# Joining two bursts of small matmuls per scan unit, with own tiles for one set of weights and three moved steps

## The chip, the core and the metric

The kernel runs on one NeuronCore of one Trainium2 chip. The core has five engines with a queue of instructions each: TensorE (PE: matmuls and transposes; loading of the stationary operand is listed apart as PEld), VectorE (DVE), ScalarE (ACT), GpSimd (POOL) and SyncE (SP, which here only issues DMAs). They run side by side and wait for each other by semaphores. The metric is the device time of one execution in microseconds: the median of the runs.

## The reference: what is computed

One decoder layer. A prompt of 2048 tokens (width 1024) and 8 single new tokens of a sample, which come with states, pass through the same layer:

```python
h = rmsnorm(x, norm_g)
p = h @ w_in                       # 8 groups of 512 columns
rq, rk, rv, rg, hq, hf, hi, hgate = split(p, 8)
# retention, 4 heads of 128: rotary on rq and rk, fixed decay per head, chunks of tokens
# HGRN2, 4 heads of 128: forget gate f = lb + (1 - lb) sigmoid(hf), per key channel
S_t = diag(f_t) S_{t-1} + k_t v_t^T ;  o_t = S_t^T q_t
y = x + concat(headnorm(o_ret) * silu(rg), headnorm(o_hg) * silu(hgate)) @ w_out
return rmsnorm(y, final_norm_g), and the last states
```

All inputs and outputs are float32.

## The kernel before, in words

**Precision.** A large product `x @ w` is made of three matmuls: both operands are split into a rounded half `h` (ACT, line 117) and a remainder `l` (DVE, line 118), and `hh + hl + lh` is accumulated. Small float32 matmuls are written once and appear as two instructions each.

**Start.** `wu` (lines 82 to 86) is a product of ones that nobody reads: 14 wide matmuls of 128 columns and 12 small ones run while the first inputs arrive.

**Value stage** (`v_pair`, line 383 on, and the loop from line 908). For three sets of projection weights (values; rotary q and its gate; rotary k and the HGRN2 gate) eight pairs of 128 tokens are taken through a 2 x 2 block product with seven instead of eight half-size products (operands `S1` to `S4` and `T1` to `T4` are sums and differences). One pair is seven steps of 12 matmuls (128x128 by 512); `after[n]` lists what is issued behind step n, and n + 0.5 means in the middle of the next step. The first two pairs are done plainly (`plain_k`), and `decode_values` multiplies the 8 sample tokens with the raw value weights `wr` in two bursts: k = 0, 1, 4, 5 after `kk = 1`, and k = 2, 3, 6, 7 after `kk = 3`. `four` spreads such a product over four column tiles. Afterwards `w_sums` (lines 502 to 507) turns the raw weights in place into the T operands.

While set 0 or 1 runs, the weights of the next set are prepared in four steps (k = 0 to 3, at pairs j = 2 to 5): `wg_load` asks SP for two pieces of 512 KB into the shared ring `raw` of six buffers, at step 0; `wg_decode` multiplies the sample tokens with them and `wg_spool` makes and stores the sums, both at step 4 (at step 5 in pair 3). The token statistics of later pairs are loaded and summed by `stats_load`, `stats_sum` and `stats_end` (POOL), and spread over partitions by a transpose (`spread`, line 288) that scales the next pair's tokens.

In the last set the retention recurrence runs along in `r_steps` (lines 795 to 828): `r_flip` transposes a chunk of rotated keys (line 726), then `r_score`, `r_update` and `r_out` follow.

**Scan stage** (`hgrn_proj`, `hgrn_rec`, `merge`). Eight units: two halves of 1024 tokens by four HGRN2 heads. The projections of unit i (`seg_steps`, line 1032, steps of six matmuls) are the filling, in which the recurrence of unit i - 1 (`levels`) and the end of unit i - 2 (`rest`) are put at given fractions of its length. A recurrence goes through seven levels of spans (1, 2, 4 ... 64 tokens), whose scores are bursts of tiny 128x32 matmuls: `scores0` (64 instructions, line 1264), `levels2(1)` and `levels2(3)` (128 each, line 1246) and `scores3` (64, lines 1289 and 1297). Between them `update(li)` multiplies keys and queries on DVE (lines 1216 and 1219) by the span products that `products` has made, and `keep` copies them on ACT. After `scores3` the score matrix `A` (one buffer) is completed by ACT; `k0` and `k1` transpose the keys (line 1107), `u0` and `u1` make the state updates, `o0` and `o1` the outputs.

**Output stage** (`out_steps`, `o_pair`). The first four chunks fill the last unit; then six pairs run through seven steps each. The sample's own output is put between them by `wd_at`: `d_ms`, `d_rs` (DVE, line 1392), `d_tr` (a transpose, line 1396) and later the products `wd_mm`.

**Order.** PE's instructions run in the order in which they are written. The other engines' order is found by a planner that simulates the program, with the rule that what stands in `behind(...)` is not issued before the instructions traced last on its engine.

Of the kernel before, what the change touches and what calls it, by code (L numbers as in the profile page):

```python
# [10 lines left out]
F32 = mybir.dt.float32  # L11
# [7 lines left out]
P = 128  # L19
# [22 lines left out]
def step_kernel(ctx, tc, a, out):  # L42
# [40 lines left out]
    for n in range(14):  # L83
        pe.matmul(wu, ones, ones, start=True, stop=True)
    for n in range(12):
        pe.matmul(wu[:32, :16], ones[:, :32], ones[:, :16], start=True, stop=True)
# [415 lines left out]
    def w_sums(r0, r1):  # L502
        dve.tensor_tensor(r0[:, 0], r0[:, 1], r0[:, 0], op=ALU.subtract)
        dve.tensor_tensor(r0[:, 1], r1[:, 1], r0[:, 1], op=ALU.subtract)
        dve.tensor_tensor(r1[:, 1], r1[:, 1], r0[:, 0], op=ALU.subtract)
        dve.tensor_tensor(r1[:, 0], r1[:, 0], r1[:, 1], op=ALU.subtract)
        return ("T2", r1[:, 1]), ("T3", r0[:, 1]), ("T1", r0[:, 0]), ("T4", r1[:, 0])
# [13 lines left out]
    def wg_decode(n, k):  # L521
        if n not in pgd:
            pgd[n] = ps_o.tile([P, 256], F32, tag="o", name=f"pgd{n}")
        for kk in (k, k + 4):
            four(pgd[n], xs[:, kk], wr[kk].rearrange("p a b -> p (a b)"), kk == 0, kk == KT - 1)
# [61 lines left out]
    def four(ps, x, w, first, last):  # L587

        for j in range(4):
            pe.matmul(ps[32 * j : 32 * j + x.shape[1]], x, w[:, j * 256 : j * 256 + 256], start=first, stop=last)  # L590
# [204 lines left out]
    def r_steps(p):  # L795
# [112 lines left out]
    for i in range(2, n_tok):  # L908
# [268 lines left out]
    MOVE = {(0, 0, 1): 0.065, (0, 1, 3): 0.065, (0, 2, 1): 0.065, (1, 0, 1): 0.125, (1, 3, 1): 0.11}  # L1177

    def hgrn_rec(half, h, u):
# [23 lines left out]
        def products():  # L1203
            box["fp"] = pools["ep"].tile([P, HALF], F32, tag="fp", name=f"fp{name}")
            for li in range(len(LEVELS)):
                two = spans(li).rearrange("p (n two) -> p n two", two=2)
                dve.tensor_tensor(spans(li + 1), two[:, :, 0], two[:, :, 1], op=ALU.mult)
            box["dec"] = sm.tile([P, CH], F32, tag="dec", name=f"dec{name}")
            dve.tensor_copy(box["dec"], spans(len(LEVELS)))
# [48 lines left out]
        def scores0():  # L1258
            box["Ab"] = pools["up"].tile([P, CH, 32], F32, tag="Ab", name=f"Ab{name}")
            pa = ps_lv.tile([P, CH, 2, 32], F32, tag="lv", name=f"pa{name}")  # L1260
            for c in range(CH):
                for i in range(4):
                    cc = slice(c * P + 32 * i, c * P + 32 * i + 32)
                    pe.matmul(pa[32 * i : 32 * i + 32, c], k[:, cc], u["qq"][:, :, cc], start=True, stop=True)
            update(0)
# [3 lines left out]
            put(pa[:, :, 1].rearrange("p c (n two b) -> p c n two b", two=2, b=1)[:, :, :, 1, :], 0)  # L1269
            keep(1)  # L1270
# [11 lines left out]
        def scores3():  # L1282
            pl = ps_lv.tile([P, CH // 2, 96], F32, tag="lv", name=f"pl{name}5")
# [9 lines left out]
            for n in range(CH // 2):  # L1293
                for g in range(4):
# [5 lines left out]
                    )  # L1300
            update(6)
# [4 lines left out]
            for e in range(2):  # L1306
                act.activation(A[0:64, e::2, 64:128], pl[64 * e : 64 * e + 64, :, 32:96], AF.Copy)
            for i in range(4):
# [25 lines left out]
        return levels, rest  # L1334
# [228 lines left out]
    levels, rest, late = [], [], []  # L1563
    tail = r_steps(N_V)
    tail_f = [lambda n=n: [f() for f in tail[n]] for n in sorted(tail)]
    for i in range(len(order)):
# [24 lines left out]
        levels, rest = hgrn_rec(*order[i], u)  # L1591
# [285 lines left out]
    wd_at[2] += [(0, d_ms), (2, d_rs), (4, d_tr)]  # L1877
# [103 lines left out]
```

## Time and profile before

| | |
|---|---|
| median of 3 runs | 1027.93 us (1026.58 to 1029.33) |
| the profiled execution | 1030.97 us |
| its span on the core | 1029.1 us |
| granted TensorE clock, mean | 0.998 |
| PE busy | 1014.0 us (99%), 8366 matmuls |
| DVE, ACT, POOL busy | 734.2, 550.3, 122.8 us |
| DMA | 255.63 MB, mean 248 GB/s |

The profile shows one execution. Its times count from the span's start; "idle before" is the time in which an engine did nothing ahead of an instruction, with what ended that wait. Matmuls are pipelined, so a row's length is longer than its distance to the next row; the distance of the starts is what one costs. By the order of time, the last product of the value stage begins at 567.75 us, the projections of the scan (L1032) at 572.75, the first recurrence burst (L1264) at 603.28, and the first product of an output pair (L350) at 901.13.

### The profile page before, as it was taken

The page shows a single profiled execution, that of the slowest core. Times are in us where ns is not written, and L with a number is a line of the kernel's source. Part 1 is how long each engine was busy: PE and PEld are TensorE (multiplying, and loading weights), DVE is VectorE, ACT ScalarE, POOL GpSimd, SP SyncE. Part 2 cuts the span into 40 slices and gives each one's busy share as a digit, 9 for nine tenths or more (in the row PEclk, how much of TensorE's full clock was granted, in tenths as well). Part 3 has the DMA queues.
Part 4 walks back from the last instruction along what each step waited for, and adds up shares of the span by engine and source line. Part 5 has one row for each costly group of instructions (what it writes and reads, how often), then busy time and mean ns, then how long its engine had stood idle before and what let it go on. Part 6 is the DMA issues. An engine that isn't in the chain of part 4 may idle for free.

```text
span 1029.1 us, 21541 instructions
## 1 busy us (share of the span) xinstructions
PE 1014.0 (99%) x8366; PEld 841.7 (82%) x8366; DVE 734.2 (71%) x1353; ACT 550.3 (53%) x1211; POOL 122.8 (12%) x231
## 2 busy tenths in 40 slices
PE   9999999999999999999999999999999999999997
PEld 7767778887778888888888899898888878878775
DVE  7887666888675885576666768768768576667886
ACT  7863435735434765555564665667556476433242
POOL 0200001000000101111111100111022112301122
PEclk9999999999999999999999999999999999999999
DMA  8699998878999965567766697555864496565652
GB/s 290 210 327 330 332 334 275 326 263 313 312 326 304 359 238 184 189 226 247 233 222 205 210 334 268 193 185 200 283 216 133 129 362 227 180 252 204 227 186 103
DMA packets 151271, 255.63 MB, mean 248 GB/s; under 512 B 11424, under 2 KB 79280, under 8 KB 151040
## 3 DMA queue, kind: packets, MB, share of 16 engines
q1 hardware_dynamic: 141408, 225.03, 64.7%
q0 software_dynamic: 7440, 24.76, 6.3%
q10 hardware_dynamic: 2320, 4.46, 1.2%
q8 instruction: 66, 1.08, 0.4%
q14 instruction: 37, 0.30, 0.1%
HBM read 166.51 MB, written 87.69 MB: 247 GB/s over the span
## 4 chain that ended last, share of the span: by engine, by line
PE 82%; DMA 4%; DVE 1%; issue 0%; SPq 0%; POOLq 0%; ACT 0%; POOL 0%; DVEq 0%; ACTq 0%
PE po L350 10%; PE pjqh L1032 9%; PE pjfh L1032 8%; PE py L1659 4%; PE plh L1246 2%; PE pur L741 1%; PE par L734 1%; PE puh L1115 1%; PE por L747 1%; PE por L749 1%; PE poh L1131 1%; DMA oT1h<-t_dramh 1%; PE poh L1133 1%; PE pv20a L350 1%; PE pv21a L350 1%; PE pv22a L350 1%
## 5 line engine op out<-in xcount | busy, mean ns | idle before, releaser
L1032 PE MATMUL pjfh<-xh,w_h 128*128 128x512 f32 (+2 forms) x160 | 59.4, 372 | 0.0
L1032 PE MATMUL pjqh<-xh,w_h 128*128 128x512 f32 (+2 forms) x160 | 58.9, 368 | 0.0
L1226 ACT ACTIVATE kepth<-kh 128x1024 f32<-128x1024 f32 x24 | 25.4, 1060 | 62.0 <-DVE kh L1216 62.0
L1032 PE MATMUL pjqh<-xh,w_l 128*128 128x512 f32 (+2 forms) x160 | 55.7, 348 | 0.0
L1032 PE MATMUL pjfh<-xh,w_l 128*128 128x512 f32 (+2 forms) x160 | 55.7, 348 | 0.0
L1032 PE MATMUL pjfh<-xl,w_h 128*128 128x512 f32 (+2 forms) x160 | 55.6, 348 | 0.0
L1032 PE MATMUL pjqh<-xl,w_h 128*128 128x512 f32 (+2 forms) x160 | 55.6, 347 | 0.0
L1216 DVE TENSOR_TENSOR kh<-kh,fph 128x512 f32<-128x512 f32 x48 | 33.4, 696 | 22.8 <-PE plh L1246 19.8
L118 DVE TENSOR_TENSOR ab_l<-xr,ab_h 128x512 fp32r<-128x512 f32 (+1 forms) x40 | 37.5, 954 | 11.6 <-ACT ab_h L117 11.6
L772 DVE SCALAR_TENSOR_TENSOR obr<-por,omr,rg 128x128 f32<-128x128 f32 x64 | 18.0, 344 | 33.3 <-POOL omr L764 28.2
L762 ACT ACTIVATE obr<-por 128x128 f32<-128x128 f32 x64 | 16.8, 277 | 44.4 <-PE por L749 40.6
L117 ACT ACTIVATE ab_h<-xr 128x512 fp32r<-128x512 f32 (+1 forms) x40 | 32.4, 838 | 11.3 <-DVE xr L302 11.3
L1032 PEld LDWEIGHTS pjqh<-xh,w_h 128*128 128x128 f32 x160 | 30.4, 190 | 4.8 <-issue 1.2
L1032 PEld LDWEIGHTS pjfh<-xh,w_h 128*128 128x128 f32 x160 | 30.2, 189 | 4.1 <-issue 0.4
L1032 PEld LDWEIGHTS pjqh<-xh,w_l 128*128 128x128 f32 x160 | 30.1, 188 | 4.1
L1032 PEld LDWEIGHTS pjfh<-xh,w_l 128*128 128x128 f32 x160 | 30.1, 188 | 4.0
L409 ACT ACTIVATE vo<-vo 128x512 f32<-128x512 f32 x32 | 20.1, 629 | 24.7 <-DVE vo L403 10.8
L1219 DVE TENSOR_TENSOR qqh<-qqh,fph 128x512 f32<-128x512 f32 x48 | 32.8, 683 | 0.0
L1032 PEld LDWEIGHTS pjqh<-xl,w_h 128*128 128x128 f32 x160 | 30.2, 189 | 3.0
L1032 PEld LDWEIGHTS pjfh<-xl,w_h 128*128 128x128 f32 x160 | 30.2, 189 | 2.7
L302 DVE SCALAR_TENSOR_TENSOR xr<-xr,g_in,rb 128x256 f32<-128x256 f32 x64 | 27.1, 480 | 7.3 <-DMA xr<-in_x_t 4.2
L1659 PE MATMUL py<-woh,oc_h 128*128 128x512 f32 x64 | 26.6, 415 | 0.0
(1839 smaller groups left out, 3335.0 us busy)
## 6 DMA issues: line engine op xcount, KB each, us to landing
xr<-a_dram SPq DMA_DIRECT2D x24, 512.0 KB
S<-s_dram SPq DMA_DIRECT2D x24, 512.0 KB
xn<-in_x_prompt SPq DMA_DIRECT2D x32, 256.0 KB
xr<-in_x_t SPq DMA_DIRECT2D x16, 512.0 KB
a_dram<-xr SPq DMA_DIRECT2D x16, 512.0 KB
s_dram<-S SPq DMA_DIRECT2D x16, 512.0 KB
wgr<-in_w SPq DMA_DIRECT2D x16, 512.0 KB
xr<-a_dram SPq DMA_DIRECT2D x32, 256.0 KB
```

Of the source, the lines that this page charges most:

```text
L117: act.activation(h, src, AF.Copy)
L118: dve.tensor_tensor(l, src, h.bitcast(F32), op=ALU.subtract)
L302: dve.scalar_tensor_tensor(r[:, k], r[:, k], g_in[:, kk : kk + 1], spread_to[i], op0=ALU.mult, op1=ALU.mult)
L350: pe.matmul(ps, xx, ww, start=(first and n == 0), stop=(last and n == 2), skip_group_check=more)
L409: act.activation(o, src, AF.Silu)
L772: dve.scalar_tensor_tensor(o[:, cc], po[:, h], ms[:, h : h + 1], rb_of[c, "g"][:, cc], op0=ALU.mult, op1=ALU.mult)
L1032: pe.matmul(ps, ww[:, kk], x[:, k, b0 : b0 + n], start=(k == 0 and i == 0), stop=(k == KT - 1 and i == 2),)
L1216: dve.tensor_tensor(kv[:, :, 0, :], kv[:, :, 0, :], two[:, :, 1:2].to_broadcast([P, nb, b]), op=ALU.mult)
L1219: dve.tensor_tensor(qv[:, :, 1, :], qv[:, :, 1, :], two[:, :, 0:1].to_broadcast([P, nb, b]), op=ALU.mult)
L1226: act.activation(ss[:, 512:], k[:, :HALF], AF.Copy)
L1246: pe.matmul(dst[32 * i : 32 * i + 32, c], kk, qq, start=True, stop=True)
L1659: pe.matmul(ps, o[:, kk], w[:, k % 4, i * 512 : (i + 1) * 512], start=(k == 0 and n == 0), stop=(k == KT - 1 and n == 2),)
```

## The change

Six edits:

- Warm-up: 5 wide matmuls and 59 with 8 columns, for 14 and 12 with 32 columns.
- `decode_values` for all eight k in one burst after `kk = 3`.
- Raw weights of the first prepared set (`n == 1`): for even k both pieces, for odd k the second piece go to tiles that already exist in the pool `vq` (`zh0`, `zl0`, `zh1`, `zl1`, and `rk`, `rg`), each piece as two DMAs of half a row. They are asked for earlier, k = 0 behind step 1 of pair 2 and k = 1 to 3 behind step 5 of pairs 2 to 4; `wg_decode` and `wg_spool` of this set move from step 4 to step 6.
- `stats_sum(i + 2, 0)` and `stats_load(i + 2, 1)` at step 1 for every pair; `r_flip(0)`, `r_score(0)` and `r_update(0)` half a step later; `d_tr` from step 4 of output pair 2 to step 0 of output pair 3.
- Scan: `scores3` of a unit is issued directly ahead of the matmuls of the next unit's `scores0`. Its end (`update(6)` and the copies into `A`) is issued behind them, ahead of `update(0)`; `k0` and `k1` follow at 0.13 and 0.16, `u0` and `u1` at 0.27 and 0.35. The copies of `Ab` into `A` go behind `levels2(3)`. The last unit keeps its own `scores3`.
- Scan, with it: the two uppermost span products are made after `scores0` (`FIRST = 5`) in one lasting tile `fp`; the places of `levels2` change (`AT`, `MOVE`).

```diff
-    for n in range(14):
+    for n in range(5):
         pe.matmul(wu, ones, ones, start=True, stop=True)
-    for n in range(12):
-        pe.matmul(wu[:32, :16], ones[:, :32], ones[:, :16], start=True, stop=True)
+    for n in range(59):
+        pe.matmul(wu[:8, :16], ones[:, :8], ones[:, :16], start=True, stop=True)
...
     def wg_load(n, k):
-        for kk in (k, k + 4):
-            wr[kk] = rawp.tile([P, 2, GW], F32, tag="raw", name=f"wgr{n}{kk}")
-            sp.dma_start(wr[kk].rearrange("p g n -> p (g n)"), a[f"w_{n}"][kk])
+        for j, kk in enumerate((k, k + 4)):
+            if n == 1 and (j or k % 2 == 0):
+                tags = ("rk", "rg") if k % 2 else (f"zh{j}", f"zl{j}")
+                wr[kk] = [vq.tile([P, GW], F32, tag=t, name=f"wgr{n}{kk}{t}") for t in tags]
+                for g, r in enumerate(wr[kk]):
+                    sp.dma_start(r, a[f"w_{n}"][kk, :, g * GW : (g + 1) * GW])
+            else:
+                wr[kk] = rawp.tile([P, 2, GW], F32, tag="raw", name=f"wgr{n}{kk}")
+                sp.dma_start(wr[kk].rearrange("p g n -> p (g n)"), a[f"w_{n}"][kk])
...
-        if kk % 2:
-            for k in (kk - 1, kk, kk + 3, kk + 4):
+        if kk == 3:
+            for k in range(KT):
                 decode_values(k)
...
-            d = 0 if p else 0.5
+            d = 0 if p else 1
             put(3.5 + d, lambda: r_flip(ca))
-            put(4 + d if p else 6, lambda: r_load(ca, "g"))
+            put(4 if p else 6, lambda: r_load(ca, "g"))
...
-            after[1 if i == 2 else 2] += [lambda i=i: behind(lambda: stats_sum(i + 2, 0)), lambda i=i: stats_load(i + 2, 1)]
+            after[1] += [lambda i=i: behind(lambda: stats_sum(i + 2, 0)), lambda i=i: stats_load(i + 2, 1)]
...
             if 2 <= j < 6:
-                after[0] += [lambda m=m, k=j - 2: wg_load(m, k)]
-                after[5 if i == 3 else 4] += [lambda m=m, k=j - 2: wg_decode(m, k), lambda m=m, k=j - 2: wg_spool(m, k)]
+                if m == 1:
+                    if j == 2:
+                        after[1] = [lambda m=m: behind(lambda: wg_load(m, 0))] + after[1]
+                    if j < 5:
+                        after[5] += [lambda m=m, k=j - 1: behind(lambda: wg_load(m, k))]
+                else:
+                    after[0] += [lambda m=m, k=j - 2: wg_load(m, k)]
+                after[6 if m == 1 else 4] += [lambda m=m, k=j - 2: wg_decode(m, k), lambda m=m, k=j - 2: wg_spool(m, k)]
...
-    MOVE = {(0, 0, 1): 0.065, (0, 1, 3): 0.065, (0, 2, 1): 0.065, (1, 0, 1): 0.125, (1, 3, 1): 0.11}
+    AT, FIRST = {1: 0.37, 3: 0.65}, 5
+    MOVE = {(0,0,1):-.12,(0,1,1):.05,(0,1,3):-.05,(0,3,0):-.068,(0,3,3):-.05,(1,0,1):.03,(1,0,3):.07,(1,1,1):.11,(1,2,0):-.068,(1,2,3):-.1}
...
         def scores0():
             box["Ab"] = pools["up"].tile([P, CH, 32], F32, tag="Ab", name=f"Ab{name}")
+            if before:
+                before["begin"]()
             pa = ps_lv.tile([P, CH, 2, 32], F32, tag="lv", name=f"pa{name}")
             for c in range(CH):
...
+            if before:
+                before["end"]()
             update(0)
...
+            products(FIRST, len(LEVELS))
             keep(1)
...
-        levels = [(0.0, products), (0.07, scores0), (0.32 + MOVE.get((half, h, 1), 0), then_decode(1, lambda: levels2(1))), (0.4, lambda: behind(load)),
-                  (0.58 + MOVE.get((half, h, 3), 0), then_decode(3, lambda: levels2(3))), (0.84, scores3),
-                  (0.95, t["k0"]), (0.98, t["k1"])]
-        rest = [(0.02, begin), (0.13, t["u0"]), (0.28, t["u1"]), (0.43, t["o0"]), (0.47, t["o1"]),
-                (0.53, t["n0"]), (0.59, t["n1"]), (0.65, t["t0"]), (0.73, t["t1"]), (0.73, last)]
+        early = [(0.0, lambda: products(0, FIRST)), (0.07 + MOVE.get((half, h, 0), 0), scores0),
+                 (AT[1] + MOVE.get((half, h, 1), 0), then_decode(1, lambda: levels2(1))), (0.4, lambda: behind(load)),
+                 (AT[3] + MOVE.get((half, h, 3), 0), then_decode(3, lambda: levels2(3))), (AT[3] + MOVE.get((half, h, 3), 0) + 0.03, scores_ab)]
+        if final:
+            levels = early + [(0.84, lambda: (scores3(), scores3_end())), (0.95, t["k0"]), (0.98, t["k1"])]
+            rest = [(0.02, begin), (0.17, t["u0"]), (0.3, t["u1"])]
+        else:
+            levels = early
+            m = max(MOVE.get((*order[order.index((half, h)) + 1], 0), 0), 0)
+            rest = [(0.02, begin), (0.13 + m, t["k0"]), (0.16 + m, t["k1"]), (0.27 + m / 2, t["u0"]), (0.35, t["u1"])]
+        rest += [(0.43, t["o0"]), (0.47, t["o1"]), (0.53, t["n0"]), (0.59, t["n1"]), (0.65, t["t0"]), (0.73, t["t1"]), (0.73, last)]
...
-    wd_at[2] += [(0, d_ms), (2, d_rs), (4, d_tr)]
+    wd_at[2] += [(0, d_ms), (2, d_rs)]
+    wd_at[3] += [(0, d_tr)]
```

`w_sums`, `wg_decode` and `four` take a raw piece as one tile or as a list of its two halves.

More of the change, by code (lines that the diff above doesn't have):

```diff
@@ L502, in w_sums @@
     def w_sums(r0, r1):
[L503 to L507, printed above, removed]
+        b11, b12, b21, b22 = (r[:, g] if hasattr(r, "shape") else r[g] for r in (r0, r1) for g in range(2))
+        dve.tensor_tensor(b11, b12, b11, op=ALU.subtract)
+        dve.tensor_tensor(b12, b22, b12, op=ALU.subtract)
+        dve.tensor_tensor(b22, b22, b11, op=ALU.subtract)
+        dve.tensor_tensor(b21, b21, b22, op=ALU.subtract)
+        return ("T2", b22), ("T3", b12), ("T1", b11), ("T4", b21)
     def wv_comb(k):
@@ L524, in wg_decode @@
         for kk in (k, k + 4):
-            four(pgd[n], xs[:, kk], wr[kk].rearrange("p a b -> p (a b)"), kk == 0, kk == KT - 1)
+            halves = wr[kk] if isinstance(wr[kk], list) else [wr[kk][:, g] for g in range(2)]
+            four(pgd[n], xs[:, kk], halves, kk == 0, kk == KT - 1)
     def wg_spool(n, k):
@@ L589, in four @@
         for j in range(4):
-            pe.matmul(ps[32 * j : 32 * j + x.shape[1]], x, w[:, j * 256 : j * 256 + 256], start=first, stop=last)
+            ww = w[j // 2] if isinstance(w, list) else w[:, j // 2 * 512 : j // 2 * 512 + 512]
+            pe.matmul(
+                ps[32 * j : 32 * j + x.shape[1]], x, ww[:, j % 2 * 256 : j % 2 * 256 + 256], start=first, stop=last
+            )
     pvd = []
@@ L1175, in keep_state, with hgrn_rec @@
         return old
-    MOVE = {(0, 0, 1): 0.065, (0, 1, 3): 0.065, (0, 2, 1): 0.065, (1, 0, 1): 0.125, (1, 3, 1): 0.11}
-    def hgrn_rec(half, h, u):
+    AT, FIRST = {1: 0.37, 3: 0.65}, 5
+    MOVE = {(0,0,1):-.12,(0,1,1):.05,(0,1,3):-.05,(0,3,0):-.068,(0,3,3):-.05,(1,0,1):.03,(1,0,3):.07,(1,1,1):.11,(1,2,0):-.068,(1,2,3):-.1}
+    def hgrn_rec(half, h, u, before):
+        final = (half, h) == order[-1]
         name = f"h{half}{h}"
@@ L1282, in scores3 @@
         def scores3():
-            pl = ps_lv.tile([P, CH // 2, 96], F32, tag="lv", name=f"pl{name}5")
+            box["pl"] = pl = ps_lv.tile([P, CH // 2, 96], F32, tag="lv", name=f"pl{name}5")
             ss = box["kept"]
@@ L1300, in scores3, with scores3_end @@
                     )
+        def scores3_end():
+            pl = box["pl"]
             update(6)
@@ L1561, in step_kernel @@
     }
-    levels, rest, late = [], [], []
+    levels, rest, late, joint = [], [], [], None
     tail = r_steps(N_V)
@@ L1590, in step_kernel @@
         late = rest
-        levels, rest = hgrn_rec(*order[i], u)
+        levels, rest, joint = hgrn_rec(*order[i], u, joint)
     fg = pools["tp"].tile([P, D], F32, tag="fg", name="fg", bufs=1)
```

16 lines of the change are left out of this document (10 added, 6 removed).

## The prediction

> **What bounds it.** I read the page's head first, then who TensorE (PE) waited for, then PE's instructions in order of time around each place that the diff touches.
>
> ```profile
> span 1029.1 us, 21541 instructions
> PE 1014.0 (99%) x8366; PEld 841.7 (82%) x8366; DVE 734.2 (71%) x1353; ACT 550.3 (53%) x1211; POOL 122.8 (12%) x231
> ```
>
> PE is never free for long, so a microsecond is gained only where PE is made to stop, or where its busy time is no work. The waits of PE, in total, times, longest:
>
> ```profile
> PE pgd L590 <- DMA wgr<-in_w: 2.7, 5, 0.7
> PE pkt L726 <- DVE rk L375: 1.4, 1, 1.4
> PE pdt L1396 <- DVE do L1392: 1.2, 1, 1.2
> PE prs L288 <- POOL rs_all L114: 0.6, 1, 0.6
> ```
>
> The diff moves something at all four. The second kind of loss is the change of shape, here from projections (L1032, 128x128) to a burst of column tiles (L1264, 128x32) and back. Columns: start, length, engine, line, what, count.
>
> ```profile
> 631.21 0.39 PE L1032 MATMUL pjfh<-xl,w_h 128*128 128x512 f32 x1
> 631.44 0.39 PE L1032 MATMUL pjfh<-xh,w_l 128*128 128x512 f32 x1
> 631.76 1.10 PE L1264 MATMUL pah<-qqh,kh 128*32 128x64 f32 x64
> 632.79 0.50 PE L1032 MATMUL pjfh<-xh,w_h 128*128 128x512 f32 x1
> 633.12 0.40 PE L1032 MATMUL pjfh<-xl,w_h 128*128 128x512 f32 x1
> ...
> L1264 PE MATMUL pah<-qqh,kh 128*32 128x64 f32 x512 | 8.8, 221 | 0.0
> ```
>
> Projections follow each other every 0.23 us (631.21 to 631.44). The burst should have begun at 631.67 and began at 631.76: 0.09 lost. Its last matmul, 0.22 long, began at 632.86 - 0.22 = 632.64, and the next projection at 632.79: 0.15, of which one step is work. The projection after that came 0.33 later, not 0.23: 0.10. One burst carries 0.09 + 0.14 + 0.10 = 0.33 us that are no work, about 0.32 with rounding.
>
> **Joint bursts.** `scores3` of a unit moves from 0.84 of the next unit's projections into the `scores0` burst of that unit; both are 128x32, so one change in and one out fall away at seven of eight units (the last keeps its own): 7 x 0.32 = **-2.3 us**. No matmul is removed. Its follow-ups move along: `update(6)` on the vector engine (DVE), six copies into `A` on ACT, then transposes `k0`, `k1` at 0.13 and 0.16 where they had stood at 0.95 and 0.98, and `u0`, `u1` at 0.27 and 0.35. Behind the joint burst DVE has this to do, in the trace after a burst of today:
>
> ```profile
> 665.39 1.23 DVE L118 TENSOR_TENSOR w_l<-wr,w_h 128x1024 fp32r<-128x1024 f32 x1
> 667.33 0.70 DVE L1216 TENSOR_TENSOR kh<-kh,fh 128x512 f32<-128x512 f32 x1 [0.71 <-PE pah L1264]
> 667.94 0.69 DVE L1219 TENSOR_TENSOR qqh<-qqh,fh 128x512 f32<-128x512 f32 x1
> 668.54 0.42 DVE L1266 TENSOR_TENSOR Abh<-pah,pk 128x256 f32<-128x256 f32 x1
> 668.99 0.45 DVE L1252 COPY_PREDICATED Abh<-lmask,pah 128x128 f32<-128x128 uint8 x1
> ```
>
> The fill advances in steps of six matmuls (6 x 0.23 = 1.4 us); 0.07 falls after two of them, 0.13 and 0.16 after three. So `k0` comes 1.4 us after the burst and needs the k half of `update(6)`, 0.6 us by these rows (667.33 to 667.94). That half depends on `scores3` alone, which ends 0.9 us (64 x 14 ns, by the 64 that start between 631.76 and 632.64) before the joint burst does; DVE stood idle 0.71 us at this place. It is in time if it runs first. The bounds for these new places are 0 and 2.4 us per unit (the slow rival below); nearest is the idle row, so I take **+0.5 us** for all seven.
>
> **Decode values.** Two bursts of 32 instructions become one of 64 two steps later: one change of shape less, **-0.3 us** by the figure above. What it moves costs more. The differences of the raw weights (L503 to L506) overwrite `wr`, which these matmuls read:
>
> ```profile
> 18.55 1.91 PE L590 MATMUL pvd<-wvr,pk 128*8 128x256 f32 x32
> ...
> 19.59 1.28 DVE L503 TENSOR_TENSOR wvr<-wvr 128x512 f32<-128x512 f32 x2
> ...
> 35.14 0.69 DVE L118 TENSOR_TENSOR T2l<-wvr,T2h 128x512 fp32r<-128x512 f32 x1 [0.60 <-ACT T2h L117]
> ...
> 38.30 0.69 DVE L118 TENSOR_TENSOR T3l<-wvr,T3h 128x512 fp32r<-128x512 f32 x1 [0.66 <-ACT T3h L117]
> ...
> 40.75 0.69 DVE L118 TENSOR_TENSOR T1l<-wvr,T1h 128x512 fp32r<-128x512 f32 x1 [0.56 <-ACT T1h L117]
> ...
> 45.02 0.69 DVE L118 TENSOR_TENSOR T4l<-wvr,T4h 128x512 fp32r<-128x512 f32 x1 [0.56 <-ACT T4h L117]
> ...
> 50.21 0.42 DVE L290 COPY rb<-prs 128x256 f32<-128x256 f32 x1 [1.34 <-PE prs L288]
> ...
> 57.96 1.23 DVE L118 TENSOR_TENSOR ab_l<-xr,ab_h 128x1024 fp32r<-128x1024 f32 x1 [1.29 <-ACT ab_h L117]
> ...
> 59.24 0.50 PE L350 MATMUL pv2b<-wv_h,ab_l 128*128 128x512 f32 x1 [0.40 <-DVE ab_l L118]
> ```
>
> Today DVE starts them at 19.59, behind the first burst. Nine such steps (0.6 each) are done before 32; afterwards none can start before about 32, when five of eight k of the joint burst are through. 5.4 us of DVE work move behind it. The gaps shown take up 0.60 + 0.66 + 0.56 + 0.56 + 1.34 = 3.7. The rest, 1.7 us, makes `rb` late, and with it the operands of pair 2, for which PE waits already (0.40 at 59.24). Ahead of them DVE idles another 1.29 us for ACT's half; if that takes up what is left nothing remains to speak of, if it is a fixed lag 1.7. I take **+0.7 us**, bounds 0 and, if no gap takes up anything, 5.4.
>
> **First set's weights.** Today each pair of raw 512 KB pieces is asked for at step 0 of a pair and used at step 4 (5 at i = 3); the change asks some five steps or more ahead, in tiles of its own, and uses it at step 6. A late burst, and one of the second set that is not:
>
> ```profile
> 70.80 0.39 PE L350 MATMUL pv2a<-T3h,s20l 128*128 128x512 f32 x1
> 71.59 0.62 PE L590 MATMUL pgd<-wgr,pk 128*8 128x256 f32 x8 [0.40 <-DMA wgr<-in_w]
> 72.80 0.62 PE L590 MATMUL pgd<-wgr,pk 128*8 128x256 f32 x8 [0.60 <-DMA wgr<-in_w]
> 73.35 0.50 PE L350 MATMUL pv2c<-B22h,s21h 128*128 128x512 f32 x1
> ...
> 236.80 0.39 PE L350 MATMUL pv10a<-T3h,s100l 128*128 128x512 f32 x1
> 237.11 1.05 PE L590 MATMUL pgd<-wgr,pk 128*8 128x256 f32 x16
> 238.09 0.50 PE L350 MATMUL pv10c<-B22h,s101h 128*128 128x512 f32 x1
> ```
>
> From the product before to the one behind: 2.55 us and 1.29, so 1.26 lost where the profile counts 1.0 as idle. All of it: 2.7 x 1.26 = **-3.4 us**. Today's four steps of 2.7 us (12 x 0.23) were up to 1.3 too short, so about 12 us are enough; the new loads have five steps (13.6) for k = 0 and eight for the others. Six of eight pieces now go as two half-row DMAs each, six more issues on SP's queue; each waits for the last reader of its tile, `a21` of the pair before, or the stored sums of k = 0, asked for six steps ahead. The sums run on DVE two steps later; their stores now stand behind the `xn` load of step 5, not ahead of it. Behind them on SP's queue is the next pair's `xn` load, held up by the four sums, 2.4 us, where the statistic is wanted a pair later. Bounds: 0 and -3.4.
>
> **Three moved steps.** `stats_load(i+2, 1)` goes from step 2 to 1, out from behind the token stores that wait for DVE on the same queue: the 0.6 of `prs`, **-0.6** (0 if the load is late for DMA's sake). `r_flip(0)` moves half a step, six matmuls, with `r_score` and `r_update` behind it: 1.36 of the 1.4 of `pkt`, **-1.3**. `d_tr` moves three steps of 2.7 us: the 1.2 of `pdt` goes, but what is late next is T3's split, used two steps after that place:
>
> ```profile
> 915.54 2.01 ACT L117 ACTIVATE oT3h<-oT3l 128x1024 fp32r<-128x1024 f32 x2 [2.60 <-DMA oT3l<-t_dramr]
> ...
> 916.63 2.36 DVE L118 TENSOR_TENSOR oT3l<-oT3l,oT3h 128x1024 fp32r<-128x1024 f32 x2 [0.71 <-ACT oT3h L117]
> ```
>
> It ends at 918.99, just when PE gets there now (916.25 + 12 x 0.23). A PE 1.2 us earlier meets its first half in time and waits a little for the second: **-1.0**, bounds -1.2 and 0.
>
> **Warm-up.**
>
> ```profile
> 1.13 3.14 PE L84 MATMUL wu<-ones 128*128 128x128 f32 x13 [1.13 <-POOL ones L78]
> ...
> 4.72 1.06 PE L84 MATMUL wu<-ones 128*128 128x128 f32 x8
> ...
> 6.05 0.93 PE L86 MATMUL wu<-ones 128*32 128x16 f32 x24
> 6.93 0.49 PE L350 MATMUL pv<-wv_h,ab_h 128*128 128x512 f32 x1
> 7.66 0.50 PE L350 MATMUL pv<-wv_l,ab_h 128*128 128x512 f32 x1 [0.23 <-DVE wv_l L118]
> ```
>
> The second product waits for `wv_l` at 7.66 however the warm-up ends, so a shorter one gains nothing. The new one has 10 wide instructions (to about 3.5) and 118 small ones. At 0.93/24, at most 0.039 each, these end by 8.1; then the second product comes 0.8 late. An 8-column load that costs a quarter of 32 columns makes it 0. I take **+0.1**, nearer the free end, because PE needs to be through only by about 7.3. [...]
>
> **Sum.** -2.3 + 0.5 - 0.3 + 0.7 - 3.4 - 0.6 - 1.3 - 1.0 + 0.1 = -7.6 us. The profiled execution took 1030.97 us (span 1029.1 and 1.9 around it), so it would take 1023.4; it lies 3.0 above the median of the runs, 1027.93, which becomes **1020.3**.
>
> **Rivals.** (1) *DVE stays late after the joint decode burst.* For it: the four gaps may be ACT's own pace and stay. Against: ACT is idle there too. Then 5.4 instead of 0.7: 1025.0. (2) *The loads only change places in a full DMA system*, and PE waits for tokens or statistics instead of weights; -3.4 and -0.6 are lost: 1024.3. Against it: no PE wait here names another load. (3) *The clock rises late.* Rows above: 13 wide ones in 3.14 us, later 8 in 1.06, half the pace until about 4.5. If 2.4 us of wide work and then tiny ones don't lift it, it rises some 3.4 us (1.13 to 4.5) after 6.93: half of 3.4 lost, and small ones at half pace end later by about 0.8: 1020.3 + 2.5 = 1022.8. [...] (4) *The queue behind the joint burst*, the slow side: at `k0` of seven units PE waits for `update(6)`, because the planner lets DVE run `update(0)`, the mask steps (667.33 to 669.44, 2.1) and the weight split (1.2) first: 2.1 + 1.2 + 0.6 - 1.4 = 2.5 us a unit, 17.5 in all, less the 0.5 counted: 1037.3. It decides from (7.6 + 0.5)/7 = 1.2 us a unit. Against it stands the 0.71 idle.
>
> **Chances.** Forecast 0.62 (by itself 1017.0 to 1023.0), rival 1 0.12, rival 2 0.09, rival 3 0.11, rival 4 0.06. About 0.3%, 3 us, is what a measurement of this kernel can tell from no change. Faster by more needs under 1024.8: the forecast, rival 3 and half of 1 and 2, which end at that edge, 0.84; same is their other half, 0.10; slower is rival 4, 0.06. The range runs from the sum with its four costs at nothing (0.5, 0.7, 0.1 and T3's 0.2), the 0.40 of pair 2 gone and the runs' own 1.4 below their median, 1017.0, up to rival 1, 1025.0.
>
> **What would show it.** Right: seven stretches where L1289, L1297 and L1264 follow without L1032 between; one `pvd` row of 64; no PE wait on `wgr`, `rk`, `do`, `rs_all`. Wrong: PE waits on `kh` or `ksh` at L1107 and L1115 (rival 4), `ab_l` or `s` waits over 1 us near 58 (rival 1), L350 at half pace after 7 (rival 3), new waits on `xr` or `xn` (rival 2).

## The result, and the profile after

The changed kernel takes 1041.63 us (median of four runs, 1040.72 to 1042.2); the kernel before took 1027.87 us beside it. The ratio is 1.0132, with a 95% interval of 1.0117 to 1.0147: 13.8 us slower, where 1020.3 us was forecast. The profiled execution took 1042.2 us.

The head of the page after, with its row of the granted clock (40 slices of 26 us, in tenths):

```profile
span 1040.4 us, 21710 instructions
PE 1016.3 (98%) x8442; PEld 845.2 (81%) x8442; DVE 730.9 (70%) x1353; ACT 551.7 (53%) x1211; POOL 133.0 (13%) x231
PEclk9999999899999999999999999999998999999999
```

The span grew by 11.3 us, less than the 13.8 between the medians, because the execution profiled before took 3.0 us more than its median. PE executes 76 matmul records more than before (8442 against 8366): the warm-up. Two slices show an 8 in the clock row. Whom PE waited for, in total, times and longest:

```profile
PE pd L599 <- DVE obh L1163: 4.3, 1, 4.3
PE pjqh L1049 <- ACT qqh L1102: 3.1, 3, 1.5
PE pv8a L350 <- ACT s L390: 1.8, 1, 1.8
PE pv8b L350 <- ACT wv_h L117: 1.6, 2, 0.9
```

The waits on `wgr`, `rk` and `do` are gone, as forecast. So is the one on the statistics (`rs_all`) at 105.63 us, but another of 1.0 us on them, at 50.99 us, has come ahead of pair 2. New ones stand in their place. Setting the start of each matmul after against its start before gives a table by stretch:

| stretch | after minus before, us |
|---|---|
| start to pair 8 (set 0) | -2.65 |
| pair 8 | +8.6 |
| rest of the value stage (`r_flip` in it) | -1.2 |
| scan | +7.6 |
| output stage | -1.2 |
| sum | +11.1 |

Two places carry most of the loss, and a third adds to it.

**Pair 8.** It is the first pair of set 1, and its second step multiplies with B21. Columns: start, length, engine, line, what, idle before and its releaser.

```profile
182.70 0.51 PE L350 MATMUL pv8b<-wv_h,ab_h 128*128 128x512 f32 x1 [0.66 <-ACT wv_h L117]
183.96 0.50 PE L350 MATMUL pv8b<-wv_l,ab_h 128*128 128x512 f32 x1 [0.75 <-DVE wv_l L118]
...
186.31 0.50 PE L350 MATMUL pv8b<-wv_h,ab_h 128*128 128x512 f32 x1 [0.91 <-ACT wv_h L117]
187.57 0.50 PE L350 MATMUL pv8b<-wv_l,ab_h 128*128 128x512 f32 x1 [0.76 <-DVE wv_l L118]
...
191.06 0.80 PE L350 MATMUL pv8a<-T2h,s70h 128*128 128x512 f32 x1 [1.79 <-ACT s L390]
191.66 0.63 PE L350 MATMUL pv8a<-T2l,s70h 128*128 128x512 f32 x1
192.08 0.63 PE L350 MATMUL pv8a<-T2h,s70l 128*128 128x512 f32 x1
```

Five stretches of idle, and behind them matmuls 0.43 us apart (191.66 to 192.08) in place of 0.23. The windows view says why (window, length, five engines, granted clock, DMA share, GB/s):

```profile
178.00:188.00 10.00, 6.92 (x27) 4.62 (x26) 2.94 (x3) 3.86 (x4) 1.09 (x2) 1.00 1.04 414
188.60:195.40 6.80, 5.01 (x12) 3.47 (x11) 6.80 (x7) 6.19 (x8) 0.00 (x0) 0.50 0.95 324
```

So some 5 us of idle were followed by 6.8 us at half the clock, which loses another 3.4. ACT, which splits B21, names the cause; first after, then before:

```profile
181.59 1.06 ACT L117 ACTIVATE wv_h<-wg1B 128x1024 fp32r<-128x1024 f32 x1 [7.08 <-DMA wg1B<-in_w]
185.20 1.06 ACT L117 ACTIVATE wv_h<-wg1B 128x1024 fp32r<-128x1024 f32 x1 [2.55 <-DMA wg1B<-in_w]
```

```profile
177.07 1.05 ACT L117 ACTIVATE wv_h<-wg1B 128x1024 fp32r<-128x1024 f32 x1
180.97 1.06 ACT L117 ACTIVATE wv_h<-wg1B 128x1024 fp32r<-128x1024 f32 x1 [2.84 <-DMA wg1B<-in_w]
```

ACT took up the third and fourth load of `wg1B` (the two pieces of B21) 4.5 and 4.2 us later, while PE came 2.65 us earlier. On SP's queue, after and then before:

```profile
161.10 0.92 SPq L324 DMA_DIRECT2D s_dram<-S  x2
...
164.53 1.11 SPq L577 DMA_DIRECT2D wg1B<-in_w  x2
...
171.05 0.30 SPq L547 DMA_DIRECT2D dg_dram<-gd  x1
171.40 2.38 SPq L577 DMA_DIRECT2D wg1B<-in_w  x4
```

```profile
157.54 0.39 SPq L569 DMA_DIRECT2D wg1B<-in_w  x1
160.20 1.52 SPq L324 DMA_DIRECT2D s_dram<-S  x2
...
164.43 0.47 SPq L569 DMA_DIRECT2D wg1B<-in_w  x1
...
165.68 0.38 SPq L569 DMA_DIRECT2D wg1B<-in_w  x1
169.75 0.30 SPq L539 DMA_DIRECT2D dg_dram<-gd  x1
```

Before, the first of the six loads went ahead of the stores of `S`, which wait for DVE, and the third ahead of the store of the decode gate, which waits for ACT. After, the first stands behind the one and the third behind the other. The planner turned the order round. The DMA engines show what that did: between 158 and 164 us their share was 0.95 before and 0.57 after, and from 164 to 184 us it was 0.99 to 1.04 after (0.85 to 1.00 before), so what was asked for later was also moved in fuller traffic. The fourth load was issued only some 1.5 us later than before and still came 4.2 later; how much of that is order and how much traffic was not separated.

**Unit (1,1).** `MOVE` puts `levels2(1)` of this unit, and the product `pd` of head 5 behind it, at 0.48, just behind `o0` (0.43) and `o1` (0.47). PE, then DVE:

```profile
791.76 0.70 PE L1268 MATMUL plh<-qqh,kh 128*32 128x16 f32 x62
796.77 1.08 PE L599 MATMUL pd<-dS,dqp 128*32 128x256 f32 x8 [4.31 <-DVE obh L1163]
797.79 0.79 PE L1049 MATMUL pjqh<-xh,w_h 128*128 128x512 f32 x1
798.38 0.63 PE L1049 MATMUL pjqh<-xl,w_h 128*128 128x512 f32 x1
```

```profile
795.00 0.68 DVE L1241 TENSOR_TENSOR qqh<-qqh,fp 128x512 f32<-128x512 f32 x1
795.60 1.12 DVE L1163 SCALAR_TENSOR_TENSOR obh<-poh,orsh,v 128x128 f32<-128x128 f32 x4
```

`pd` needs one of the two banks of the PSUM pool `o`. Both hold an output of `o0` and `o1`, and the first is emptied by `n0` (L1163), which DVE does only behind the updates of `levels2`. DVE was not short of time: what `n0` needs was ready at 791.17 us, when POOL had finished, and DVE stood idle until it got the first of these updates:

```profile
790.13 1.04 POOL L114 TENSOR_TENSOR orsh<-orsh,mhalf 128x4 f32<-128x4 f32 x1
792.51 0.69 DVE L1238 TENSOR_TENSOR kh<-kh,fp 128x512 f32<-128x512 f32 x1 [4.49 <-PE plh L1268]
```

`n0` stands at 0.53 in `behind(...)`, so it can't go ahead of what `levels2(1)` put on DVE at 0.48. Before, `levels2(1)` and `pd` stood at 0.32, ahead of `o0`, and `pd` did not wait:

```profile
780.18 0.62 PE L590 MATMUL pd<-dS,dqp 128*32 128x256 f32 x6
...
782.24 0.38 PE L1131 MATMUL poh<-v,Ah 128*128 128x128 f32 x2
```

In the changed kernel PE idles 4.3 us, and 6.8 us of half clock (796.1 to 803.0) follow: 7.6 us.

**Smaller.** Three evictions of `q` come late, because ACT does the copies of `Ab` first, which the change put right behind `levels2(3)`:

```profile
661.61 1.68 ACT L1342 ACTIVATE Ah<-Abh 32x256 f32<-32x256 f32 x4
663.32 1.26 ACT L1172 ACTIVATE oth<-poth,pk 128x512 f32<-128x512 f32 x2
664.47 0.87 ACT L1102 ACTIVATE qqh<-pjqh 128x512 f32<-128x512 f32 x2
```

**The joint bursts themselves** do what the diff says, in all seven units. One of them:

```profile
634.77 0.39 PE L1049 MATMUL pjfh<-xh,w_l 128*128 128x512 f32 x1
635.09 0.46 PE L1316 MATMUL plh<-kepth 128*32 128x32 f32 x32
635.36 0.66 PE L1324 MATMUL plh<-qqh,kh 128*32 128x64 f32 x31
...
635.84 1.09 PE L1288 MATMUL pah<-qqh,kh 128*32 128x64 f32 x63
636.86 0.50 PE L1049 MATMUL pjfh<-xh,w_h 128*128 128x512 f32 x1
```

### The profile page after: what moved, and what is told of

Same layout as the page of the kernel before. It is cut to its first block, busy times and chain, and to the rows that moved or that the text cites. A ratio compares the mean times of both kernels' runs of the same rounds, so it can differ in the third digit from the quotient of the medians.

```text
span 1040.4 us, 21710 instructions
## 1 busy us (share of the span) xinstructions
PE 1016.3 (98%) x8442; PEld 845.2 (81%) x8442; DVE 730.9 (70%) x1353; ACT 551.7 (53%) x1211; POOL 133.0 (13%) x231
## 3 DMA queue, kind: packets, MB, share of 16 engines
q8 instruction: 66, 1.08, 0.4%
## 5 line engine op out<-in xcount | busy, mean ns | idle before, releaser
L1238 DVE TENSOR_TENSOR kh<-kh,fp 128x512 f32<-128x512 f32 x48 | 33.0, 688 | 20.4 <-PE plh L1268 14.3
L1241 DVE TENSOR_TENSOR qqh<-qqh,fp 128x512 f32<-128x512 f32 x48 | 32.8, 684 | 0.0
L1154 ACT ACTIVATE jkh<-poh 128x128 f32<-128x128 f32 x64 | 17.7, 277 | 18.6 <-PE poh L1150 17.3
```

Source lines behind the costliest of these rows:

```text
L1154: act.activation(jk, po[:, j], AF.Square, accum_out=ms[:, j : j + 1])
L1238: dve.tensor_tensor(kv[:, :, 0, :], kv[:, :, 0, :], two[:, :, 1:2].to_broadcast([P, nb, b]), op=ALU.mult)
L1241: dve.tensor_tensor(qv[:, :, 1, :], qv[:, :, 1, :], two[:, :, 0:1].to_broadcast([P, nb, b]), op=ALU.mult)
```

## The experiments

Each was timed beside the kernel before, on the same chip (its medians there lie between 1027.65 and 1028.26 us).

### Halves: a third cause appears

*Scan part alone*, and *all but the scan part*, each taken from the diff as it stands. The scan part is everything from `AT, FIRST` to the call of `hgrn_rec`; the other half is what is left (`wu`, `decode_values`, the weights, `r_flip`, the statistics, `d_tr`):

```diff
-    def hgrn_rec(half, h, u):
+    def hgrn_rec(half, h, u, before):
...
+    AT, FIRST = {1: 0.37, 3: 0.65}, 5
...
-        levels, rest = hgrn_rec(*order[i], u)
+        levels, rest, joint = hgrn_rec(*order[i], u, joint)
```

> Only the scan part of the change (joint bursts, new places, split products, the copies of Ab), the rest as before. Theory A, two places: the changed scan loses 7.6 us where the product pd waits for a PSUM bank in unit (1,1), half of it as a lower clock, and elsewhere it is even: 1027.9 + 7.6 = 1035.5 us, with one stretch of half clock of about 6.8 us near 787 us and a PE wait pd <- DVE obh of about 4 us. Theory B, the scan is what failed everywhere (queues behind the joint bursts): 1040 us or more, waits spread over all units. Theory C, the scan is right by itself and is only hit by the late start: 1026 us.

> The change without its scan part. Theory A: value stage +4.6, output stage -1.2, so 1027.9 + 3.4 = 1031.3 us, one stretch of half clock near 189 to 195 us, and PE stalls of about 6 us in pair 8 for wv (from the late loads wg1B). Theory B: the gains of the small steps remain, 1020 to 1022 us, and pair 8 is as before.

Measured: scan part alone 1039.52 us, ratio 1.0119 (1.0099 to 1.0139); the rest 1040.93 us, 1.0128 (1.0101 to 1.0156). Both miss. The `pd` wait and the half clock are where theory A had them in the first, and the late B21 in the second, but each half costs nearly as much as the whole. In the first, theory A had also left out the three waits on `q` (3.1 us). The waits of the second show an entry that neither kernel had:

```profile
PE plh L1263 <- issue: 3.9, 2, 3.2
PE pd L599 <- issue: 2.4, 1, 2.4
...
PE pjfh L1049 <- issue: 1.4, 1, 1.4
```

"issue" is time in which PE waits for nothing that the profile shows. All of it lies inside level bursts or just behind one; in these a matmul starts every 9 to 15 ns in the mean. Counting PE's instruction records (weight loads, matmuls, its own semaphore instructions) from the start up to each of these stretches, and dividing by 256, leaves a remainder of 192 at all four (idle from 618.9, 691.5, 762.9 and 872.9 us), and 193 at the one of the scan part alone (from 608.2). And the trace lists 66 transfers of 16 KiB of the kind "instruction" (1.08 MB), about one for 256 of PE's 17000 instructions. The author reads this as PE waiting for its own code, in blocks of 256: a block of 256 instructions lasts 15 to 30 us among wide matmuls (128 of them at 0.12 to 0.23 us) and can last 1 to 3.6 us around a burst.

### Where the code blocks end

The warm-up adds 152 instructions (76 matmuls, each with its weight load) ahead of everything, so by this count it shifts every block end. *Warm-up alone*:

```diff
-    for n in range(14):
+    for n in range(5):
         pe.matmul(wu, ones, ones, start=True, stop=True)
-    for n in range(12):
-        pe.matmul(wu[:32, :16], ones[:, :32], ones[:, :16], start=True, stop=True)
+    for n in range(59):
+        pe.matmul(wu[:8, :16], ones[:, :8], ones[:, :16], start=True, stop=True)
```

> Only the new warm-up in the kernel before: 5 wide and 59 tiny matmuls for 14 wide and 12, which is 76 more matmul records (152 instructions) at the start, all else as before. Theory F, code blocks: every idle stretch of PE that the profile of the run without the scan part puts down to issue lies at the same place modulo 256 of PE's instruction count (192), where the block before it took under 3.5 us; the shift of 152 instructions moves these places into the level bursts, so the scan loses some 9 us: 1027.8 + 9.6 = 1037.4 us (1034 to 1040), with PE waits on issue in L1246 bursts. Rival, as the prediction had it (warm-up +0.1, nothing else moves): 1028 us and no PE wait on issue over 0.5 us.

Measured: 1036.49 us, ratio 1.0072 (1.0045 to 1.0099). The warm-up, whose matmuls nobody reads and which ends in time, costs 8.2 us through places 600 us later. The profiled execution, at 1033.86 us the fastest of the four, shows 4.9 us of such stops and a stretch of half clock of 3.41 us (1.7 us lost). Its largest PE wait in the list, and the same in order of time:

```profile
PE plh L1246 <- issue: 2.9, 2, 2.5
```

```profile
862.24 0.62 PE L1246 MATMUL plh<-qqh,kh 128*32 128x16 f32 x52
865.39 0.30 PE L1246 MATMUL plh<-qqh,kh 128*32 128x16 f32 x10 [2.54 <-issue]
```

The burst stops ten matmuls before its end, and goes on 1.44 us after the one 16 KiB transfer of that stretch (863.07 to 863.95) is through. At the ten such stops of four kernels this distance was 1.24 to 1.57 us.

*Scan part and warm-up together* (the two diffs above, nothing else):

> The scan part and the new warm-up together, nothing else of the change. Alone the scan part cost 11.8 us over before (1039.5) and the warm-up 8.2 us (1036.5). Theory F, code blocks: the 152 instructions of the warm-up put the block ends back where no block is shorter than 3.9 us with the joint bursts, so that only pd's bank wait and the waits of pjqh are left: 1027.8 + 7.6 = 1035.5 us (1034 to 1037), less than the scan part alone, and no PE wait on issue over 0.5 us. Rival, costs that add up: 1027.8 + 11.8 + 8.2 = 1047.8 us.

Measured: ratio 1.0101 (1.0058 to 1.0144), runs of 1036.0, 1038.8 and 1042.1 us (one of 5.8 ms is left out). The costs do not add up to 1047.8: the two parts need each other, and the short blocks are gone. But the lowest run alone reaches what theory F gave; in the profiled one a block of nearly 5 us still ran dry for 3.1 us: its transfer started over 5 us after the block before had ended. In the scan stage of the 14 traces the median of this distance is 1.0 to 2.0 us, but it scatters, and now and then reaches 5 us without a stop. By kernel, from the traces:

| kernel | blocks under 3.6 us | of these with a stop | stops at longer blocks |
|---|---|---|---|
| before | 0 (shortest 3.9) | | 0 |
| after | 0 (shortest 4.3) | | 0 |
| scan part alone | 6 | 1 | 0 |
| all but the scan part | 6 | 4 | 0 |
| warm-up alone | 6 | 4 | 0 |
| scan part and warm-up | 0 (shortest 4.1) | | 1 |
| entry (1,1,1) taken out | 1 | 0 | 0 |
| three repairs together | 1 | 0 | 0 |

The last two kernels come further down, and the six that are not listed have neither short blocks nor stops. Stops stand mostly at short blocks: 9 of 20 stop, and of all the longer ones a single one. That a block stops when its transfer starts late is the author's estimate; what decides which of them stop, and what delays a transfer, was not shown. For the change as a whole the code blocks explain nothing of the 13.8 us: its profile has no wait of PE on issue.

### Pair 8

*B11 and B21 asked for earlier*, first with the decode gate put off by three steps (the last two lines), then without these:

```diff
                 for n, (_, op, _) in enumerate(CHAIN):
-                    after[n] = [lambda m=m, op=op: wg_fetch(m, op)] + after[n]
+                    if m > 1 or n > 1:
+                        after[n] = [lambda m=m, op=op: wg_fetch(m, op)] + after[n]
+            if m == 1 and j == 6:
+                for n, at in ((0, 4), (1, 6)):
+                    after[at] += [lambda m=m, op=CHAIN[n][1]: wg_fetch(m, op)]
...
-                after[0] += [lambda m=m: behind(lambda: wg_decode_out(m))]
+                after[3 if m == 1 else 0] += [lambda m=m: behind(lambda: wg_decode_out(m))]
```

> The changed kernel with the loads of B11 and B21 of the first prepared set asked for some steps earlier in program order, and the store of the decode gate asked for three steps later, so that on SP's queue the third and fourth load stand ahead of that store. Theory A, head of the line on SP: the four loads are issued by about 167 us and not by 172, the last of B21 lands near 180 us and not at 185.2, pair 8 loses at most 1.5 us and keeps full clock: 1041.6 - 7.5 = 1034.1 us. Rival, the DMA system is full between 164 and 190 us whatever the order, the loads land as late as now: 1041 us, half clock near 189 us as before.

> As the run with the loads of B11 and B21 asked for earlier, but the store of the decode gate stays at its step, so that its two buffers of the ring vo come free as early as in the changed kernel. Theory A (late loads make pair 8 stall): no PE wait on wv of over 1 us in pair 8, none of 4.8 us on vo, full clock there: 1040.7 - 7.5 = 1033 to 1035 us. Rival: the DMA system is full and something else of the same length is late there: 1040 us or more.

Measured: 1041.34 us (1.0134, 1.0114 to 1.0154) and 1037.28 us (1.0089, 1.0060 to 1.0118). In both the stalls of pair 8 are gone. In the first, one of the same length stands in pair 7:

```profile
PE pv7a L350 <- ACT vo L402: 4.8, 1, 4.8
```

The gate's two tiles (`gd`) come from the ring `vo` of three. Their store was issued at 175.72 us, now behind five loads of 512 KB, and the next ACT eviction into that ring ran at 181.29. That the ring is what it waited for is read from the code and these times; the run with all repairs bears it out. In the second run 2.7 us of it are left; with 1.2 us on another eviction and 3.41 us of half clock behind them, pair 7 loses 5.9 us there, which is why that run misses the 1033 to 1035 us expected of it.

*The weights' edit alone* (`w_sums`, `wg_load`, `wg_decode`, `four` and their steps, on the kernel before):

```diff
+                if m == 1:
+                    if j == 2:
+                        after[1] = [lambda m=m: behind(lambda: wg_load(m, 0))] + after[1]
+                    if j < 5:
+                        after[5] += [lambda m=m, k=j - 1: behind(lambda: wg_load(m, k))]
...
+                after[6 if m == 1 else 4] += [lambda m=m, k=j - 2: wg_decode(m, k), lambda m=m, k=j - 2: wg_spool(m, k)]
```

> Only the edit of the first set's raw weights (loads into tiles of their own, earlier; decode and sums at step 6) in the kernel before. Theory A: this edit alone turns the order on SP's queue round (the first load of B11 behind the stores of S and v and not ahead of them), so pair 8 stalls: the 2.7 us of wgr waits go (3.4 with what goes with them) and pair 8 loses 5 to 8.6 us with half clock behind it: 1027.8 - 3.4 + 7 = 1031 us (1029 to 1033). Rival: pair 8 fails because PE comes 2.65 us earlier through all edits together, the order alone does nothing: 1024.5 us and full clock up to the end.

Measured: 1029.9 us, ratio 1.0016 (1.0003 to 1.0030). Theory A falls in this form: pair 8 runs at full clock, the third load still stands ahead of the gate's store (165.18 and 169.47), and the last piece of B21 lands at 180.39. The rival falls too: PE reaches pair 8 only 0.22 us earlier than in the kernel before. Most of the 3.4 us gained on `wgr` is lost again to other waits of the same pairs, on statistics and on an eviction:

```profile
PE prs L288 <- POOL rs_all L114: 1.6, 3, 0.5
PE pv2c L350 <- ACT p L390: 1.3, 1, 1.3
```

*The changed kernel with the statistics' load back at its old step*:

```diff
-            after[1] += [lambda i=i: behind(lambda: stats_sum(i + 2, 0)), lambda i=i: stats_load(i + 2, 1)]
+            after[1 if i == 2 else 2] += [lambda i=i: behind(lambda: stats_sum(i + 2, 0)), lambda i=i: stats_load(i + 2, 1)]
```

> The changed kernel with the statistics load back at step 2 (step 1 only at i = 2), as before. In its order on SP the third load of wg1B (the first half of B21) stands ahead of the store of the decode gate again, while PE comes just as early to pair 8. Theory, the place in SP's queue decides: the third load lands by 177 us and the fourth by 181.5, pair 8 stalls under 1.5 us in all, with no half clock there: 1040.7 - 8 + 1.5 to 2 (the waits prs on POOL, 0.7 each in the run with the weights' edit alone, are back) = 1034.5 us. Rival, PE's being 2.65 us earlier is enough to meet the loads too soon: 1040 us, half clock near 189 us.

Measured: 1036.48 us, ratio 1.0084 (1.0057 to 1.0111). The third load is issued at 164.22, ahead of the gate's store at 168.50; both pieces of B21 are there by 177 us, pair 8 has no wait on `wv` and no half clock; three `prs` waits are back (1.6 of the 2.5 us on them; the rest, ahead of pair 2, the changed kernel has too). They bring PE to pair 8 only 1.19 us ahead of the kernel before, not 2.65, but the loads would have been in time for that too (B21 was wanted at 181.9 then). So the weights' edit puts the first load behind the stores of `S`, and only with the statistics' step does the third go behind the gate's store, which is what stalls pair 8. The statistics' step without the weights' edit was not run.

### The two places in the scan

The entry (1,1,1) is taken out of `MOVE`, and in another run the copies of `Ab` are put at 0.84 (pieces of long lines):

```diff
-(1,0,3):.07,(1,1,1):.11,(1,2,0):-.068
+(1,0,3):.07,(1,2,0):-.068
...
-(AT[3] + MOVE.get((half, h, 3), 0) + 0.03, scores_ab)]
+(0.84, scores_ab)]
```

> The changed kernel with one entry taken away, levels2(1) and the product of head 5 of unit (1,1) at 0.37 and not at 0.48, so ahead of o0 and o1. Theory A: the product finds a free PSUM bank, its 4.3 us stall and the half clock behind it go: 1041.6 - 7.5 = 1034.1 us, no pd wait over 0.5 us, one stretch of half clock left (pair 8). Rival: the product waits because DVE is late behind levels2, wherever it stands: 1041 us, the wait of about 4 us remains at another name.

> The changed kernel with the copies of Ab into A put at 0.84 of the unit and not right behind levels2(3). Theory A: the three PE waits of pjqh on ACT's eviction (3.1 us) go, 1040.7 - 3 = 1037.7 us; rival: ACT is late there for its other work (keep, evictions) and the waits stay or come back at puh or in another unit, 1040.7 us.

Measured: 1036.08 us (1.0077, 1.0061 to 1.0092) and 1039.52 us (1.0108, 1.0081 to 1.0135). The `pd` wait is gone in the first, and no stall takes its place; in the second the three waits on `q` are gone, with 0.7 us new on `qqh`. The first gives 5.6 us of the 7.5; in its profile the half clock of pair 8 lasted 10.2 us and not 6.8, which takes 1.7 us back. The second gives 2.1 us of the 3.

### A repaired version

The three repairs together, then a fourth: the decode gate in tiles of its own, and only the product of head 5 taken from 0.48 to 0.37, with `levels2(1)` left there (some of the lines are pieces), so that no code block is short (with the whole step at 0.37 one lasts a little over 2 us, though PE did not stop there).

```diff
-        t, u = (vq.tile([NB, GW], F32, tag="vo", name=f"gd{n}{ty}", bufs=3) for ty in range(2))
+        t, u = (vq.tile([P, GW], F32R, tag=f"z{'hl'[ty]}1", name=f"gd{n}{ty}")[:NB].bitcast(F32) if n == 1 else vq.tile([NB, GW], F32, tag="vo", name=f"gd{n}{ty}", bufs=3) for ty in range(2))
...
+                 (0.37, lambda: behind(lambda: d_mm(5)) if (half, h) == (1, 1) else None), (0.84, scores_ab)]
...
-    mm_at = {(1, 0, 3): [4], (1, 1, 1): [5], (1, 1, 3): [6], (1, 2, 1): [7]}
+    mm_at = {(1, 0, 3): [4], (1, 1, 3): [6], (1, 2, 1): [7]}
```

> The changed kernel with three repairs at once: loads of B11 and B21 earlier, (1,1,1) at 0.37, the copies of Ab at 0.84. If the three places explain all of it and the rest of the prediction's sum holds: 1041.6 - 7.5 - 5.5 - 3 = 1025 to 1026 us by the measured parts so far, faster than before (1027.8) by some 2 us; 1020 us if the code blocks fall well. If a stall goes elsewhere: 1030 us or more.

> The changed kernel with four repairs: B11 and B21 asked for earlier; the decode gate's two tiles taken from zh1 and zl1 and not from the ring vo of three, which it held until its store had landed; the product of head 5 alone at 0.37, with levels2(1) of (1,1) left at 0.48 so that the code blocks stay long; the copies of Ab at 0.84. Theory: the 3.8 us that pair 7 still lost to the ring vo in the run with three repairs go, and no block is under 4 us: its profiled span 1026.3 - 3.8 = 1022.5, about 1022 to 1024 us as a median, 0.5% faster than before. Rival: the DMA system is full in pairs 7 and 8 and another wait of that length takes the place: 1028 us.

Measured: 1029.6 us, ratio 1.0017 (1.0001 to 1.0033), with 3.8 us still lost in pair 7; and 1024.56 us, ratio 0.9965 (0.9950 to 0.9979). The second beats both kernels. All its PE waits of 0.5 us and more:

```profile
PE wu L84 <- POOL ones L78: 1.1, 1, 1.1
PE pah L1292 <- DVE qqh L1108: 0.7, 1, 0.7
PE puh L1136 <- ACT ksh L1130: 0.7, 1, 0.7
```

## Why the prediction was wrong, by its own steps

**What it summed comes out by the profiles.** With the four places repaired, the profiled span is 1021.8 us, 7.3 under the one before; the sum was -7.6. By stretch: start to pair 8 -3.2 (the terms for weights, statistics, decode values and warm-up make -3.5), `r_flip` -1.6 (-1.3), scan -2.5 (-2.3 and +0.5), output stage -1.2 (-1.0). The burst overhead and the new places near zero fit this. T3's split was not the next thing late: PE never waits for it, after or repaired, and -1.2 is that term's far bound. What the sum did not hold is 0.9 us in pair 8. By the medians less than half of the sum is there; the step from the profile to the median, below, says why.

**First set's weights: "Bounds: 0 and -3.4".** This step failed first. It followed its own loads and stores down SP's queue as far as the next `xn` load, and never asked where the next set's `wg1B` would then stand, though the order of that queue is found anew by the planner whenever anything on it moves. The bound excluded a loss; pair 8 lost 8.6. The step was right on one thing: the `wgr` waits went, all of them. Rival 2 (the waits only change places) holds for this edit alone, 1029.9 us.

**Three moved steps: "0 if the load is late for DMA's sake".** The wait that it priced (0.6 us at 105.63) is gone, and with the old step three such waits stand in these pairs (1.6 us). But with the weights' edit the statistics' step was the second half of pair 8's stall, and the bound of 0 had excluded that.

**Joint bursts: "Its follow-ups move along".** The step costed `update(6)`, six copies, `k0` to `u1`, and bounded their places by 0 and 2.4 a unit. It left out two lines of the same part: the entry (1,1,1) of `MOVE`, which brings `pd` behind `o0` and `o1` into a pool of two banks (7.6), and the copies of `Ab`, which now go ahead of the eviction of `q` (3.1). Rival 4, the queue at `k0`, did not happen: no wait on `kh` at `k0`, and 0.6 on `ksh` once.

**Warm-up +0.1.** Right for its own place: the small matmuls end at 6.7 us (118 in 3.15), and by the trace's clock record the clock rises at 4.25 (4.51 before), so rival 3 fell. Wrong as a model, since it treated the instructions as free once they were over. Alone it costs 8.2; in the change no stop is seen, and its shortest block lasts 4.3 us. The forecast was not hurt by this, but nothing in it would have noticed.

**From the profile to the median: "it lies 3.0 above the median".** This step failed too. The waits were priced on that one execution and the sum carried over whole. Other traces show the same code with less of them. In the scan part alone, whose value stage is unchanged, PE waits 2.1 us on `wgr` and 0.6 on `rk` (2.7 and 1.4 in the profile before), and the scan begins 0.93 us earlier. With the warm-up alone the three waits on `wgr`, `rk` and `do` are 1.5, 0.4 and none (2.7, 1.4 and 1.2), and the scan begins 2.86 us earlier. So the terms -3.4, -1.3 and -1.0, read from that one execution, were most likely too large for a median. The repaired kernel gains 7.3 us between profiles, but 3.1 between medians (1027.65 to 1024.56; 3.6 by the ratio), and its profiled run was in turn the lowest of its six. Going by the repaired kernel, the change without its stalls was worth some 3 us and not 7.6; that the sum and the repaired profile agree so well is in part luck.

The chance given to slower, 0.06, rested on one mechanism with a price per unit; the real losses were single places.

## What to carry to other kernels

Where an order is planned anew, a moved load has to be followed on its queue to the first consumer after it that has no slack, here a set of weights two pairs later; a bound that excludes a loss needs the whole queue, not the instructions of the diff. When a product is moved, ask which accumulator bank it will take, who empties it, and what stands ahead of that on its engine: a wait of a few us can grow through the clock (here 4.3 us became 7.6). And count the instructions: 152 more at the start alone cost 8.2 us here, in bursts of tiny instructions 600 us later, so time such a change together with a count that puts the block ends back.

## What the runs showed of the hardware

**Code blocks.** In the two halves of the change, the stops of PE that the profile puts down to issue leave nearly the same remainder when PE's instructions are counted by 256 (192 at four, 193 at one). In all, ten stops of four kernels were seen, nine of them where a block took under 3.6 us (20 such blocks). PE idled 0.4 to 3.2 us at them and resumed 1.24 to 1.57 us after a 16 KiB transfer. In these bursts a matmul and its weight load take 9 to 15 ns in the mean.

**Stretches of half clock.** Ten of the 14 traces have half clock before the last microseconds of the program; each such stretch lasted 3.41, 6.83 or 10.24 us, one, two or three times 3.41. They followed one idle stretch of 2.5 us or more, or several in a row; but one of 3.1 us left the clock alone where another of 2.5 lowered it, and the same 4.3 us at `pd` brought 6.83 in five traces and 3.41 in two. What decides between these was not shown.
